# SiLU gate with loads and stores on one DMA ring instead of two

## The chip, the cores and the metric

The kernel runs on one core of a Trainium2 chip. A core has compute engines that work at the same time and wait for one another through semaphores; this kernel uses two of them, ScalarE (ACT in the profile) and VectorE (DVE). SyncE (SP) computes nothing here; it issues transfers. Data moves between the off-chip memory (HBM) and the on-chip memory (SBUF, 128 partitions) by DMA, on 16 DMA engines. A transfer is issued by an instruction of SP or ACT; its packets then stand in a ring that belongs to the issuing engine, and the DMA engines work through the rings. The profile calls the ring of SP q1 and that of ACT q10.

The metric is the time of one execution on the device, in microseconds (us). The kernel before took 471.0 us (median of three runs, 470.98 to 471.02).

## The reference

The input x has the shape 32 x 512 x 2048 in float32. The last axis is cut into two halves of 1024; the output is SiLU of the first half times the second half.

```python
half_dim = x.shape[-1] // 2
x1, x2 = x[..., :half_dim].copy(), x[..., half_dim:].copy()
silu_x1 = x1 * (1 / (1 + np.exp(-x1)))
return (silu_x1 * x2).astype(np.float32)
```

That is 134.2 MB read, 67.1 MB written, one activation and one multiply for each output element.

## The kernel before

The 32 x 512 rows are taken as 16384 rows of 2048 numbers. A tile is 1024 rows: 128 partitions with K = 8 rows each. So there are 16 tiles; a tile's load is 8 MB (64 KB in one piece for each partition) and its store 4 MB (32 KB in one piece for each partition). The helper `view` (lines 42 and 43) picks tile i of a tensor.

In SBUF there are two input buffers, `xts`, and two output buffers, `ots`; tile i uses number i % 2 of each. ACT overwrites the first half of an input row with its SiLU (line 96), and DVE multiplies the two halves into the output buffer (line 102). Both calls are in `compute`. Most tiles are one activation and one multiply of 128 x 8192 elements. Tile 0 is done in four parts of 2 rows a partition (`FIRST`), and tile 15 in parts of 2, 3 and 3 rows (`LAST`).

The order of the work is written out by hand. Every transfer goes through `move` (line 76), which issues it on the queue that it is given and notes it in `sent`. `load(i)` issues on SP and `store(i, ...)` on ACT. The order in the program is load 0, load 1, and then for each tile i: compute tile i, store tile i, load tile i+2. For tiles 4 to 7 and 12 to 15 (`load_first`) the load stands ahead of the store; for those two queues that changes the order in which the transfers take their semaphores, and not what each queue waits for.

Load i+2 writes the input buffer that multiply i reads, so SP waits for that multiply ahead of it. Store i waits on ACT's queue for the same multiply. Multiply i+2 writes the output buffer that store i reads, so it waits for that store to land. ACT's queue is in order too: the activation of tile i+1 stands behind store i.

Tile 0 is stored in three transfers (`OPENING`): every fourth partition from 0, every fourth from 2, and then every odd one. Tile 15 is stored in three transfers that follow `LAST`. All other stores are one transfer over all partitions. Loads are always one transfer.

The helper `implied` tells the framework that a dependency is already covered by another one. `after` fixes an order in the program without a wait. At the end `settle_all_but` makes SP wait for all transfers but the last, and then the program ends when the last has landed.

Of the kernel before, what the change touches and what calls it, by code (L numbers as in the profile page):

```python
# [1 line left out]

# [4 lines left out]


@with_exitstack
def kernel(  # L10
    ctx: ExitStack,
    tc: tile.TileContext,
    x: bass.AP,
    out: bass.AP,
):


    nc = tc.nc
    P = nc.NUM_PARTITIONS

    x_flat = x.flatten_outer_dims()
    out_flat = out.flatten_outer_dims()
    num_rows, in_cols = x_flat.shape
    half = in_cols // 2
    dt = x_flat.dtype

    K = 8
    FIRST = [2] * (K // 2)
    LAST = [2, 3, 3]
    OPENING = [  # L30
        (slice(0, None, 4), slice(None)),
        (slice(2, None, 4), slice(None)),
        (slice(1, None, 2), slice(None)),
    ]
    RUN = 2
    n_tiles = num_rows // (P * K)

    pool = ctx.enter_context(tc.tile_pool(name="pool", bufs=1))
    xts = [pool.tile([P, K, in_cols], dt, name=f"xt{b}") for b in range(2)]
    ots = [pool.tile([P, K, half], dt, name=f"ot{b}") for b in range(2)]  # L40

    def view(flat, i):
        return flat.rearrange("(g p t k) d -> g t p k d", p=P, t=RUN, k=K)[i // RUN, i % RUN]

    ctx.enter_context(tc.manual_schedule(engines={mybir.EngineType.Activation, mybir.EngineType.DVE}))

    sent = []
    loads, stores, silus, muls = {}, {}, {}, {}

    def implied(later, earlier, reason):  # L50
        for x in later:
            for y in earlier:
                tc.declare_no_dep(x, y, reason=reason)

    def earlier(done, i):
        return [ins for j in range(i % 2, i, 2) for ins in done[j]]

    def after(later, first):
        tc.add_manual_dep(
            later,  # L60
            first.name,
            mybir.DependencyInfo(mybir.DependencyClass.NoSync, mybir.DependencyReason.DATA),
            reason="order in which the transfers take their semaphores",
        )

    def settle_all_but(n, others):
        rest = nc.sync.nop(nofuse=True)
        for ins in sent[:-n] + others:
            tc.add_manual_dep(
                rest.ins,  # L70
                ins.name,
                mybir.DependencyInfo(mybir.DependencyClass.Sync, mybir.DependencyReason.DATA),
                reason="sync sees each earlier transfer land before the last ones",
            )

    def move(queue, out, in_):
        ins = queue.dma_start(out=out, in_=in_).ins  # L77
        sent.append(ins)
        return ins

    def load(i):
        loads[i] = [move(nc.sync, xts[i % 2][:], view(x_flat, i))]
        if i >= 2:
            implied(loads[i], earlier(loads, i), "the multiplies that this load awaits came after those loads")
            implied(loads[i], earlier(silus, i), "the multiplies that this load awaits came after those activations")

    def parts(sizes):
        assert sum(sizes) == K
        return [slice(sum(sizes[:n]), sum(sizes[:n + 1])) for n in range(len(sizes))]

    def compute(i, ot, chunks):
        xt = xts[i % 2]
        silus[i], muls[i] = [], []
        for ks in chunks:
            silus[i].append(
                nc.scalar.activation(  # L96
                    out=xt[:, ks, :half],
                    in_=xt[:, ks, :half],
                    func=mybir.ActivationFunctionType.Silu,
                ).ins  # L100
            )
            muls[i].append(nc.vector.tensor_mul(out=ot[:, ks], in0=xt[:, ks, :half], in1=xt[:, ks, half:]).ins)  # L102
        implied(muls[i], loads[i], "each multiply awaits an activation that came after the load")
        if i >= 2:
            implied(silus[i], earlier(silus, i), "the load that this activation awaits came after those activations")
            implied(silus[i], earlier(muls, i), "the load that this activation awaits came after those multiplies")
            implied(muls[i], earlier(muls, i), "the store that this multiply awaits came after those multiplies")

    def store(i, ot, pieces):
        ov = view(out_flat, i)  # L110
        stores[i] = [move(nc.scalar, ov[ps, ks], ot[ps, ks]) for ps, ks in pieces]

    ALL = slice(None)
    load(0)
    load(1)
    for i in range(n_tiles):
        ot = ots[i % 2]
        last = i == n_tiles - 1
        compute(i, ot, parts(FIRST if i == 0 else LAST if last else [K]))
        pieces = [(ALL, ALL)]  # L120
        if i == 0:
            pieces = OPENING
        elif last:
            pieces = [(ALL, ks) for ks in parts(LAST)]
        load_first = i // 4 % 2
        if load_first and i + 2 < n_tiles:
            load(i + 2)
        store(i, ot, pieces)
        if load_first and i + 2 < n_tiles:
            after(stores[i][0], loads[i + 2][0])  # L130
        if not load_first and i + 2 < n_tiles:
            load(i + 2)
            after(loads[i + 2][0], stores[i][-1])
    settle_all_but(1, muls[n_tiles - 1])


# [1 line left out]
_INS = ['x']  # L138
_OUTS = [((32, 512, 1024), 'float32')]


# [23 lines left out]
```

## Time and profile before

| | |
|---|---|
| time, median of three runs | 471.0 us |
| the profiled execution, first to last instruction (span) | 469.2 us |
| median less span | 1.8 us |
| DVE busy | 139.5 us, 21 multiplies |
| ACT busy | 114.2 us, 21 activations and one table load |
| multiply of a whole tile | 8.69 us |
| activation of a whole tile | 7.03 us |
| ring of SP (loads) | 134.22 MB, 66.4% of the span of 16 engines |
| ring of ACT (stores) | 67.11 MB, 33.2% of the span of 16 engines |
| load, from issue to landing (median) | 42.2 us |
| store of a whole tile, from issue to landing (median) | 42.0 us |

The span is one execution taken by the hardware profiler, from its first to its last instruction; that is the only time that the profile gives of that execution. The chain of waits is the chain of work that ended last, followed back from the end: each step names what released it. In a table by stretches, each row is a stretch of the span, with its length, the busy time of each engine, the mean busy share of the 16 DMA engines, and what they moved in GB/s. There, a DMA packet is counted where it starts, with its whole duration and its whole size. So in a short stretch that holds the start of one packet on each of the 16 engines, the share times the length is the mean duration of a packet, and the GB/s times the length is the size of the 16 packets.

### The profile page before, as it was taken

The numbers are of one execution on the slowest core, as the hardware profiler recorded it, in microseconds if no ns is written. First come the engines' busy times: TensorE is split into PE (matmuls) and PEld (weight loads), VectorE is DVE, ScalarE is ACT, GpSimd is POOL, SyncE is SP. The second block draws the span as 40 slices with busy tenths as digits, with TensorE's granted clock in tenths as the row PEclk, the third lists the DMA queues.
The fourth block names the chain that finished last, engine by engine and source line by source line (L and its number), as shares of the span: only waits on it lengthen the run. The fifth ranks groups of instructions, "written<-read, shape, count | busy, mean of one in ns | idle before, by whom it ended". The sixth has DMA issues, their size and how long they took to land.

```text
span 469.2 us, 156 instructions
## 1 busy us (share of the span) xinstructions
DVE 139.5 (30%) x21; ACT 114.2 (24%) x22; POOL 0.2 (0%) x4
## 2 busy tenths in 40 slices
DVE  0070522407034070330704307042070520605152
ACT  1051405032050410504105050050501405014060
POOL 0000000000000000000000000000000000000000
DMA  8999999999999999999999999999999999999998
GB/s 358 447 447 374 475 402 433 416 492 402 411 439 486 408 402 447 475 419 402 444 439 458 402 436 413 492 402 416 433 486 408 402 447 475 419 402 444 450 402 358
DMA packets 4928, 201.33 MB, mean 429 GB/s; under 512 B 576, under 2 KB 576, under 8 KB 576
## 3 DMA queue, kind: packets, MB, share of 16 engines
q1 hardware_dynamic: 2304, 134.22, 66.4%
q10 hardware_dynamic: 2624, 67.11, 33.2%
HBM read 134.22 MB, written 67.11 MB: 429 GB/s over the span
## 4 chain that ended last, share of the span: by engine, by line
DMA 72%; DVE 14%; ACT 11%; DVEq 1%; issue 0%; SPq 0%
DMA xt<-in_x_dram 72%; DVE ot L102 14%; ACT xt L96 11%; DVEq L160 1%; SPq L77 0%
## 5 line engine op out<-in xcount | busy, mean ns | idle before, releaser
L102 DVE TENSOR_TENSOR ot<-xt 128x8192 f32<-128x8192 f32 (+2 forms) x21 | 139.5, 6659 | 320.8 <-ACT xt L96 320.8
L96 ACT ACTIVATE xt<-xt 128x8192 f32<-128x8192 f32 (+2 forms) x21 | 112.9, 5400 | 341.4 <-DMA xt<-in_x_dram 341.4
L96 ACT ACT_TABLE_LOAD x1 | 1.3, 1283 | 0.7 <-PEq L149 0.7
L149 POOL MEMSET const-bfloat16-1.0<- 128x1 bf16 x1 | 0.1, 102 | 0.0
L149 POOL MEMSET const-uint8-127<- 128x1 uint8 x1 | 0.1, 102 | 0.0
L149 POOL MEMSET const-float32-0.0<- 128x1 f32 x1 | 0.1, 99 | 0.2 <-issue 0.2
L149 POOL MEMSET const-float32-1.0<- 128x1 f32 x1 | 0.1, 99 | 0.0
## 6 DMA issues: line engine op xcount, KB each, us to landing
out_dram<-ot ACTq DMA_DIRECT2D x14, 4096.0 KB, 42.0
out_dram<-ot ACTq DMA_DIRECT2D x3, 1024.0 KB, 12.0
out_dram<-ot ACTq DMA_DIRECT2D x2, 1536.0 KB, 7.9
out_dram<-ot ACTq DMA_DIRECT2D x1, 2048.0 KB, 37.2
xt<-in_x_dram SPq DMA_DIRECT2D x16, 42.2
```

The source lines that it names most:

```text
L96: nc.scalar.activation(out=xt[:, ks, :half], in_=xt[:, ks, :half], func=mybir.ActivationFunctionType.Silu,).ins
L102: muls[i].append(nc.vector.tensor_mul(out=ot[:, ks], in0=xt[:, ks, :half], in1=xt[:, ks, half:]).ins)
L149: nc = _bacc.Bacc("TRN2", target_bir_lowering=False, num_devices=1)
L160: with _tile.TileContext(nc) as tc:
```

## The change

All stores are issued by SP, as the loads are. The ring of ACT isn't used any more. For each tile, store i stands ahead of load i+2 on SP's queue, in the program and in the ring; the alternation by `load_first` is gone. The store of tile 0 is one transfer over all partitions. The three stores of tile 15 stay three.

```diff
-    OPENING = [
-        (slice(0, None, 4), slice(None)),
-        (slice(2, None, 4), slice(None)),
-        (slice(1, None, 2), slice(None)),
-    ]
...
     def store(i, ot, pieces):
         ov = view(out_flat, i)
-        stores[i] = [move(nc.scalar, ov[ps, ks], ot[ps, ks]) for ps, ks in pieces]
+        stores[i] = [move(nc.sync, ov[ps, ks], ot[ps, ks]) for ps, ks in pieces]
...
         pieces = [(ALL, ALL)]
-        if i == 0:
-            pieces = OPENING
-        elif last:
+        if last:
             pieces = [(ALL, ks) for ks in parts(LAST)]
-        load_first = i // 4 % 2
-        if load_first and i + 2 < n_tiles:
-            load(i + 2)
         store(i, ot, pieces)
-        if load_first and i + 2 < n_tiles:
-            after(stores[i][0], loads[i + 2][0])
-        if not load_first and i + 2 < n_tiles:
+        if i + 2 < n_tiles:
             load(i + 2)
             after(loads[i + 2][0], stores[i][-1])
```

## The prediction

> **What bounds the kernel now.** I read the page first: the busy shares, the rings, and the DMA issues.
>
> ```profile
> DVE 139.5 (30%) x21; ACT 114.2 (24%) x22; POOL 0.2 (0%) x4
> ...
> q1 hardware_dynamic: 2304, 134.22, 66.4%
> q10 hardware_dynamic: 2624, 67.11, 33.2%
> HBM read 134.22 MB, written 67.11 MB: 429 GB/s over the span
> ...
> out_dram<-ot ACTq DMA_DIRECT2D x14, 4096.0 KB, 42.0
> ...
> xt<-in_x_dram SPq DMA_DIRECT2D x16, 42.2
> ```
>
> Both compute engines idle more than two thirds of the span, and the packets of the two rings together fill 66.4 + 33.2 = 99.6% of what the 16 DMA engines have. So the DMA engines are the bound. The chain of waits seems to say otherwise, since it puts 25% on DVE and ACT; two tiles of it:
>
> ```profile
> 275.07 0.02 issue
> 275.09 7.04 ACT xt L96
> 282.13 0.02 issue
> 282.15 8.70 DVE ot L102
> 290.85 0.02 issue
> 290.87 42.19 DMA xt<-in_x_dram
> 333.06 0.02 issue
> ```
>
> A load takes 42.19 us from issue to landing, but that is mostly queueing. From landing to landing of tiles of one buffer it is 333.06 - 275.07 = 57.99 us, 29.00 a tile. What the engines can do in 29 us is in the table by stretches (length, DVE, ACT, POOL, clock, DMA share, GB/s):
>
> ```profile
> 1.70:2.50 0.80, 0.00 (x0) 0.31 (x1) 0.00 (x0) 1.00 3.98 1311
> 4.70:33.70 29.00, 8.90 (x4) 7.31 (x4) 0.00 (x0) 1.00 1.00 434
> 31.20:32.00 0.80, 0.80 (x2) 0.00 (x0) 0.00 (x0) 1.00 3.02 1311
> 36.10:36.90 0.80, 0.00 (x0) 0.00 (x0) 0.00 (x0) 1.00 4.10 1311
> ...
> 391.20:420.20 29.00, 8.69 (x1) 6.97 (x2) 0.00 (x0) 1.00 1.00 434
> ...
> 449.20:456.46 7.26, 5.08 (x2) 7.09 (x3) 0.00 (x0) 1.00 1.00 433
> 449.20:449.90 0.69, 0.00 (x0) 0.69 (x1) 0.00 (x0) 1.00 1.75 754
> 458.30:460.15 1.85, 1.85 (x1) 0.00 (x0) 0.00 (x0) 1.00 1.03 436
> ```
>
> The fifth row is the steady state: both rings at work, share 1.00, 434 GB/s. The second is the start, loads 0 and 1 alone on SP's ring: the same 434. The sixth is the end, store 14 alone on ACT's ring: 433. So the DMA engines move the same bytes per us whether rings alternate or one ring runs alone, and whether it reads or writes. From the short rows comes a packet: 1311 GB/s x 0.80 us is 1.05 MB, 16 packets of 64 KB. A load packet takes 3.02 x 0.80 = 2.42 us; the very first, in the first row, 3.98 x 0.80 = 3.18; the one that starts at 36.1, 4.10 x 0.80 = 3.28. A store packet takes 1.75 x 0.69 = 1.21 us.
>
> The packet at 36.1 matters. Store 0 is the first use of ACT's ring; its first part is issued at 33.53, and the load packet then under way takes 0.86 us longer than its neighbours. It happens on all 16 engines (the row's mean is over 16 packets) and does not come back: the row of the steady state has two issues in it (at 406.9) and its mean is full. Once, then, 0.86 us of DMA time is lost.
>
> **The change, part by part.**
>
> *The stores move from ACT's queue to SP's.* ACT loses 20 DMA issues, 17 of about 0.36 us and 1.86 us for the three of tile 0. They cost nothing before: ACT idles 341.4 us for loads. SP gains 18 issues of some 0.33 us, and stands idle otherwise. SP's queue now holds store i ahead of load i+2. Store i waits for multiply i, and so does load i+2 (290.87 in the chain), so the load is later by one issue, 0.33 us, which its place in the ring must cover: next point. Nothing else is queued on SP until the final waits; POOL has no transfer. On ACT, the activation of tile i+1 no longer stands behind store i, but it waits for a load that lands 13 us after that anyway.
>
> *The order in the ring.* Let load i land at time 0. Multiply i ends at 0.02 + 7.04 + 0.02 + 8.70 = 15.8, and store i and load i+2 are issued by 16.5. Ahead of them the ring holds store i-1, 8 packets x 1.21 = 9.68, and load i+1, 8 x 2.416 = 19.33 (12 packets take 29.00 in the second row), which were issued a period earlier. That is 29.01 us of work, so the ring has over 12 us left when new work comes. It doesn't run dry. Load i+2 lands at 2 x 29.01 = 58.0, as now; from issue to landing it stays 42.2. Store i lands about 13.2 + 9.7 = 23 us after issue instead of 42.0, so multiply i+2, which needs the output buffer at about 65, is still covered, by 26 us instead of 7. Per tile 29.01 in place of 29.00: over 14 tiles +0.1 us.
>
> *The opening.* Load 1 has no stores beside it and lands at 22.64 + 19.33 = 42.0 instead of 45.36. Store 0 and load 2 are in the ring by 34.2, 8 us before it ends. Store 0 as one transfer carries the same 4 MB; 32 short completion packets fewer are nothing. The 0.86 us goes if it belongs to starting the second ring, which no longer exists; it stays if it belongs to the first write of the program. The bounds are 0 and -0.86. I take -0.86, because the other slow packet, the first of SP's ring, shows a like size (3.18 - 2.42 = 0.76) where a ring starts and nothing is written; and SP's ring never empties.
>
> *The turns in one ring.* This is what the trace doesn't show: a store behind a load in the same ring (15 times) and a load behind a store (14 times). Load behind load is in the second row: it holds the border between loads 0 and 1 and is still full. Store behind store is between the sixth and last rows. Between rings, direction changes at every packet in the fifth row and costs nothing. Lower bound 0 (a full engine can't gain; the fifth row is no slower than the second); upper bound 0.86 each, the only turn in the trace that lost time, 29 x 0.86 = 25 us. I take 0, the value of the three nearest rows.
>
> Here a rule speaks against the change. The Trainium skill, "DMA: Bandwidth & Descriptors", section "Anatomy of one DMA — SWDGE (gpsimd) path", gives every transfer a fixed cost of about 2 us beside its bytes. If one ring paid that at each of 33 borders with nothing else to fill it, 66 us (an estimate from that page) would come on top. The trace contradicts it for load behind load, where the second row has no gap. The same page, section "Queues, rings and completion order", says that data descriptors of a ring carry no barrier, by which the turns are free.
>
> *The end.* After load 15 lands, store 14 (9.68 us) is in the ring; the first part of tile 15 is issued 4.3 us later (449.06 to 453.35 now), the others at 8.0 and 11.3, and the ring needs them at 9.7, 12.1 and 15.8. Nothing changes; SP then waits for all, as now.
>
> **Sum**, against the profiled execution: 469.2 - 0.86 + 0.1 = 468.4 us of span. The median lies 1.8 us above that span, and I keep that: 470.2 us, -0.16%.
>
> **Rivals.**
>
> *The loss stays (471.1 us).* It came with the first write and not with the second ring: 471.0 + 0.1. For it: a load packet was hit just when the first store came. Against: the like loss where a ring starts.
>
> *Turns cost (slower).* Each of the 29 turns inside the ring leaves the engines idle for c, because what comes next isn't prepared while the last packet of the other direction drains; two rings hid it. The time is 470.2 + 29c. It is 0.2% slower from c = (471.94 - 470.2)/29 = 0.06 us; c = 0.1 gives 473.1 and c = 0.86 gives 495.1. For it: 0.86 was lost at the first turn. Against: direction changes are free at every packet of the fifth row, and borders are free in one direction.
>
> *More than the sum (469.6 us).* Without ACT's ring something outside the span goes too. There are 1.8 us there, unseen by the profile; a third of it gives 470.2 - 0.6. Nothing in the profile speaks for it; its bounds are 468.4 and 470.2.
>
> **How the numbers follow.** The forecast gets 0.52, the loss that stays 0.15, turns 0.22, the gain outside 0.11. 0.2%, 0.94 us, is about what a measurement of this kernel can tell from no change; faster is then below 470.06 and slower above 471.94. The forecast lies 0.14 from the first: of its 0.52 I give 0.10 to faster. Of the turns' 0.22, 0.03 is c below 0.06. So faster 0.10 + 0.11 = 0.21, slower 0.19, same 0.60. The range from 469.3 to 472.6 takes in forecast, staying loss and most of the gain outside, and turns up to c = 0.08; it leaves out dearer turns (0.16) and a larger gain (0.03). The likeliest case's own range is 469.8 to 470.6.
>
> **What would show it.** Right: one ring with 201.33 MB and a share over 99%; landings of loads at 42.0, 71.0, 100.0 and 448.1 us; stores landing about 23 us after issue; per tile 29.0; the packets at 36 us at 2.42; span 468.4. The staying loss would be one load or store packet near 42 us that is 0.8 longer. Turns would show as periods of 29.0 + 2c and as shares below 1.00 in stretches around a border. The prediction is wrong if the ring runs dry after a multiply (SP's store waiting for anything but that multiply), or if the packets themselves take other than 2.42 and 1.21 us once reads and writes come in long runs.

## The result

The changed kernel takes 476.15 us (median of four runs, 476.10 to 476.83) against 471.01 us for the kernel before: the ratio is 1.0114, with a 95% interval of 1.0101 to 1.0126. The forecast was 470.2 with a range to 472.6, so it is 5.1 us slower where 0.8 us of gain was forecast. The profiled execution took 476.83 us with a span of 475.1; the other three have spans of 474.3 to 474.4.

### The profile page after: what moved, and what is told of

Read it like the earlier page. It is cut to its first block, busy times and chain, and to the rows that moved or that the text cites. A ratio compares the mean times of both kernels' runs of the same rounds, so it can differ in the third digit from the quotient of the medians.

```text
span 475.1 us, 153 instructions
## 1 busy us (share of the span) xinstructions
DVE 139.5 (29%) x21; ACT 114.2 (24%) x22; POOL 0.2 (0%) x4
## 3 DMA queue, kind: packets, MB, share of 16 engines
q1 hardware_dynamic: 4896, 201.33, 98.7%
## 4 chain that ended last, share of the span: by engine, by line
DMA 72%; DVE 14%; ACT 11%; DVEq 1%; SPq 1%; ACTq 1%; issue 0%
DMA xt<-in_x_dram 72%; DVE ot L97 14%; ACT xt L91 11%; DVEq L148 1%; SPq L72 1%; ACTq L148 1%
## 6 DMA issues: line engine op xcount, KB each, us to landing
out_dram<-ot SPq DMA_DIRECT2D x15, 4096.0 KB, 23.2
xt<-in_x_dram SPq DMA_DIRECT2D x16, 42.3
```

## The profile after

From the page of the changed kernel, in the order of the lines shown of before:

```profile
DVE 139.5 (29%) x21; ACT 114.2 (24%) x22; POOL 0.2 (0%) x4
...
GB/s 353 441 441 395 466 378 439 441 422 455 406 472 419 406 466 395 439 441 422 450 419 447 436 425 452 395 461 400 428 447 425 447 433 436 439 397 469 414 352 282
...
q1 hardware_dynamic: 4896, 201.33, 98.7%
HBM read 134.22 MB, written 67.11 MB: 424 GB/s over the span
...
out_dram<-ot SPq DMA_DIRECT2D x15, 4096.0 KB, 23.2
...
xt<-in_x_dram SPq DMA_DIRECT2D x16, 42.3
```

The plan of the change came out: one ring, the same bytes, compute untouched, whole stores landing after 23.2 us (forecast: about 23), loads after 42.3. The ring doesn't run dry in the body. Yet the rate is 424 GB/s instead of 429, and the last two slices, 352 and 282, are low. Where the time went is in the chain of waits, in the activations of tiles 1, 3, 5 and so on, each of which starts when its load has landed:

```profile
43.09 7.04 ACT xt L91
...
103.09 7.04 ACT xt L91
...
162.30 7.04 ACT xt L91
...
220.97 7.04 ACT xt L91
...
279.63 7.04 ACT xt L91
...
338.17 7.04 ACT xt L91
...
396.75 7.04 ACT xt L91
...
454.80 1.91 ACT xt L91
```

Two tiles should take 58.0 us. They take 60.00, 59.21, 58.67, 58.66, 58.54, 58.58 and 58.05. Load 1 is already 1.1 us late (42.0 forecast), and load 15 lands at 454.8 instead of the 448.1 forecast: 6.7 us, of which 1.1 come up to load 1 and 5.6 between loads 1 and 15.

The table by stretches shows what is long:

```profile
4.65:33.60 28.95, 8.90 (x4) 7.31 (x4) 0.00 (x0) 1.00 1.00 435
...
38.45:39.30 0.85, 0.00 (x0) 0.00 (x0) 0.00 (x0) 1.00 4.09 1234
43.25:50.50 7.25, 0.35 (x1) 6.87 (x1) 0.00 (x0) 1.00 1.00 434
66.30:66.95 0.65, 0.00 (x0) 0.00 (x0) 0.00 (x0) 1.00 3.49 1512
68.70:69.35 0.65, 0.00 (x0) 0.00 (x0) 0.00 (x0) 1.00 3.75 1512
...
456.00:466.00 10.00, 8.90 (x3) 6.01 (x3) 0.00 (x0) 1.00 0.80 337
471.10:473.60 2.50, 0.00 (x0) 0.00 (x0) 0.00 (x0) 1.00 0.12 49
```

Inside runs of one direction nothing changed: loads alone move 435 GB/s, stores alone 434. The second row holds the 16 last packets of load 1, right ahead of store 0: 4.09 x 0.85 = 3.48 us each, 1.06 longer than 2.42. The fourth and fifth rows hold 15 packets each (1512 GB/s x 0.65 us is 0.98 MB): the last but one and the last packet of load 2. Shares of 3.49 and 3.75 mean 2.42 and 2.60 us: the last load packet ahead of a store is longer, here by 0.18 on average.

The packet records of the whole trace (start, duration and size of each packet) show this at the turns from load to store: 1.06 us on average at the first, 0.07 to 0.20 at the others, and 0.02 at the fifteenth. Elsewhere in the body all but a handful of packets keep 1.21 and 2.42. The long packets are not the same length on all engines: at the second turn they are 0 to 0.5 us over. What decides is the slowest engine, for a tile has landed when all 16 have done their part. By the packets' start times, the first packets of store 0 start within 0.7 us of one another, those of store 13 within 6.0.

The last two rows are the price at the end. After load 15 has landed, the engines that are ahead run dry and wait for tile 15 (share 0.80; before, by the packet records, all engines were busy from there to the last 2 us), and in 2.5 us shortly before the end about two of the 16 still move something. The busy shares say the same: 99.6% of 469.2 us is 467.3 us of packets for each engine before, and 98.7% of 475.1 us is 468.9 after. So of the 5.9 us that the profiled execution is longer, about 2 are longer packets on the average engine and about 4 are engines that stand idle.

## The experiments

Every comparison is with runs of the kernel before on the same chip in the same session (470.86 to 470.99 us).

**Is it the opening?** The store of tile 0 was changed as well as the ring. First the whole store on two rings:

```diff
-            pieces = OPENING
+            pieces = [(ALL, ALL)]
```

> The kernel before with store 0 as one transfer over all partitions, on ACT's ring as before; nothing else. Theory of the turns (a DMA engine loses time each time that a store follows a load in the same ring): this kernel has no such turn before store 14, so 471.0 us, at most 0.5 away. Theory of the opening (the three parts of store 0 kept the 16 engines in step, and the whole store lets them drift apart): about 476, as the changed kernel, with loads' landings later and later.

Measured: 471.02 us, ratio 1.0008 (0.9998 to 1.0017). Then the three parts on one ring:

```diff
-        stores[i] = [move(nc.scalar, ov[ps, ks], ot[ps, ks]) for ps, ks in pieces]
+        stores[i] = [move(nc.sync, ov[ps, ks], ot[ps, ks]) for ps, ks in pieces]
...
-        load_first = i // 4 % 2
+        load_first = False
```

> The changed kernel with store 0 in the three transfers of before, all on SP's ring. Theory of the turns: 15 turns from load to store are still there, 476.1 us, at most 1 away. Theory of the opening: 471.0.

Measured: 475.47 us, ratio 1.0099 (1.0084 to 1.0114). So the opening is cleared: the whole store costs nothing on two rings, and its parts save at most 0.7 us on one.

**Is it writing at all, or many transfers in one ring?**

```diff
+        if i == n_tiles - 1:
+            stores[i] = [move(nc.sync, ov[ps, ks], ot[ps, ks]) for ps, ks in pieces]
+        else:
+            again = x_flat.rearrange("(a p h) d -> a p (h d)", p=P, h=K // 2)
+            stores[i] = [move(nc.sync, ot[:].rearrange("p k d -> p (k d)"), again[i])]
```

> The changed kernel with stores 0 to 14 replaced by reads: in their place in the ring stands a transfer of the same 4 MB in packets of the same size from x into the output buffer, so 15 of the 16 tiles of the output are not written. One ring, as many transfers, no turn to a store before the very end. Theory that the loss is at turns from load to store: 29.0 us a tile and no long packet after the first, so a span of 468.4 and 469.7 to 470.7 us. Rival, that many transfers in one ring cost, whatever their direction: 475 to 476.

Measured: 470.87 us, ratio 1.0000 (0.9991 to 1.0010), span 469.0. The time is 0.2 above the expected upper end, as every packet is a few ns longer. But at the place of the first turn there is nothing; the row answers to 38.45:39.30 above, 2.85 x 0.85 = 2.42 us:

```profile
38.45:39.30 0.85, 0.00 (x0) 0.00 (x0) 0.00 (x0) 1.00 2.85 1234
```

So 34 transfers in one ring cost nothing when all but the last three read. The loss needs stores among the loads.

**Is it a price for each turn?** Loads and stores were cut by partitions and issued in turn, so that there are more turns with shorter runs:

```diff
+    WAYS = [slice(j, None, 4) for j in range(4)]
...
+            for ps in WAYS:
+                stores[i].append(move(nc.sync, ov[ps], ot[ps]))
...
+                loads[i + 2].append(move(nc.sync, xts[i % 2][ps], xin[ps]))
```

> The changed kernel, but stores 0 to 13 and the loads behind them are each cut into four transfers of every fourth partition, issued in turn on SP's ring: a quarter store, a quarter load, and so on. The packets are the same; each DMA engine now goes from load to store 4 times a tile, 57 times instead of 15. Theory of the turns, at a price for each: the changed kernel lost 5.1 us over 15 turns, 0.34 each, so 57 give 476.1 + 42 x 0.34 = 490 us. Rival, long runs (the loss comes from 8 packets of one direction in a row, which let the engines drift apart, and not from the turns): with runs of 2 packets it falls, 471 to 473, with about 1 us for 84 more transfers (at some 0.012 us for a transfer's completion).

Measured: 473.95 us, ratio 1.0065 (1.0050 to 1.0080). With nearly four times the turns the loss is smaller, so a fixed price for a turn is out; the long-run rival came nearer, 1 us below what was measured. The chain of waits shows more than the time does:

```profile
1.17 41.74 DMA xt<-in_x_dram
42.91 0.02 issue
42.92 29.48 DMA xt<-in_x_dram
72.41 0.02 issue
72.42 29.89 DMA xt<-in_x_dram
102.31 0.02 issue
102.33 29.52 DMA xt<-in_x_dram
131.84 0.02 issue
131.86 29.02 DMA xt<-in_x_dram
160.88 0.02 issue
160.90 29.02 DMA xt<-in_x_dram
```

Three tiles lose 0.5, 0.9 and 0.5 us; from then on every tile takes 29.04, to the end. By the packets' start times the engines are then, after 11 turns, 2.0 us apart, and stay so. The same transfers with the stores on ACT's ring are the comparison:

```diff
-                stores[i].append(move(nc.sync, ov[ps], ot[ps]))
+                stores[i].append(move(nc.scalar, ov[ps], ot[ps]))
```

> The quarters of the run with four transfers each, but with the stores on ACT's ring: as many transfers, and each DMA engine alternates one load packet and one store packet. Theory of the run: no loss at the turns, 471.0 plus the completions of 84 more transfers, 0.5 to 1 us, so 471.3 to 472.2; what the one-ring kernel took above this is its loss at turns. Rival, that most of the 3 us of the one-ring kernel with quarters was the price of the extra transfers: 473.5 to 474.5.

Measured: 471.92 us, ratio 1.0022 (1.0012 to 1.0031). The extra transfers cost 0.9 us; the rest of the 3.1, about 2.0 us, is the loss on one ring.

In the kernel before, where nearly every load packet after the start stands alone between two stores, the 16 engines stay 0.6 us apart from the first turn to the end, and no later load packet is longer: turns that all engines make at nearly the same time cost nothing there.

Halves instead of quarters (`slice(j, None, 2)`):

> The changed kernel with stores 0 to 13 and the loads behind them cut into two transfers each (every second partition), issued in turn on SP's ring: runs of 4 packets of one direction, 29 turns from load to store. Theory of the run (a turn from load to store costs more the longer the run of load packets before it): between the 474.0 us measured with runs of 2 and the 476.1 us with runs of 8, so 474.4 to 475.8. Rival, a fixed price for a turn: 476.1 + 14 x 0.34 = 481 us.

Measured: 476.00 us, ratio 1.0109 (1.0079 to 1.0139), with executions from 474.4 to 477.4. That is no fixed price either, but it lies 0.2 us above the range expected and is not clearly less than the changed kernel: the loss differs by 3 us from execution to execution, and how the time grows between runs of 4 and of 8 packets can't be read from these. The packet records of the profiled executions give an order: after the first turn, load packets are longer by 0.0 us in all for each engine in the kernel before, 0.6 with quarters on one ring, 1.1 with halves and 1.9 in the changed kernel.

**Is it the ring?** One ring with the order of packets that two rings give, every eighth partition:

> The same with eight transfers each (every eighth partition): on each DMA engine one store packet, one load packet, and so on, in a single ring. That is the order of packets that the two rings of before give. Theory of the run: nothing is lost at the turns, so the time of before plus about 1 us for 196 more transfers (14 tiles x 14, each with a completion packet of 9 ns on each engine, 1.8 us at most): 471.5 to 473. Rival, the ring itself (two rings hide the turn, one doesn't): 475 or more.

Measured: 720 to 734 us, which says nothing on the question, for it made another bottleneck. A stretch of the steady state:

```profile
200.00:229.00 29.00, 2.57 (x1) 0.00 (x0) 0.00 (x0) 1.00 0.98 262
```

The engines are busy and move 262 GB/s; load packets of 64 KB take 4.47 us (median of the packet records) instead of 2.42. The Trainium skill, "SBUF — State Buffer", section "Door 1: The DMA port swizzle", maps partitions to 16 ports by bits 2 to 4 and 6 of the partition's number. Every eighth partition leaves bit 2 fixed, so by that map eight ports serve 16 engines. The trace agrees with a load packet 1.85 times as long (4.47 against 2.42 us); other causes were not tried.

So the runs were shortened by rows instead, all partitions in every transfer:

```diff
+    WAYS = [slice(j * K // 8, (j + 1) * K // 8) for j in range(8)]
...
+                stores[i].append(move(nc.sync, ov[:, ks], ot[:, ks]))
...
+                loads[i + 2].append(move(nc.sync, xts[i % 2][:, ks], xin[:, ks]))
```

> The changed kernel with stores 0 to 13 and the loads behind them cut by rows: eight transfers each of one row of every partition, issued in turn on SP's ring. Packets are 8 KB and 4 KB; a run of loads before a store is 8 packets but only about 2.5 us long, as one packet of 64 KB. Small packets cost something of their own (8 KB packets took 0.306 us at the end of the kernel before, 1.3% more than an eighth of a 64 KB packet). Theory that the length of the run in time sets the loss: within 1 us of the same kernel on two rings, which runs beside it. Rival, one ring or the number of packets in the run: 3 us or more above it.

> The same eight transfers of one row, with the stores on ACT's ring: the comparison for the kernel on one ring. Both theories: 1 to 3% above the time before from the small packets, 475 to 485 us.

Measured: 481.56 us on one ring, ratio 1.0225 (1.0210 to 1.0240), and 540.5 on two, ratio 1.1484. The second is no comparison. Its queues stopped one another; the waits of SP:

```profile
SPq L73 <- DMA xt<-in_x_dram: 254.0, 70, 14.1
```

SP waited 254 us, not for a multiply but for earlier loads to land. The kernel's transfers take eight semaphores in turn, and 16 transfers a tile use each of them twice; probably that is why the queues waited for each other, which no run tested. The DMA engines are idle at times (share of busy time 0.7 to 0.8 in 17 of 40 slices). So the expectation on the pair is untested. The kernel on one ring says something by itself. Stretches of two tiles, from the start to the end of its body:

```profile
100.00:158.00 58.00, 17.39 (x2) 14.06 (x2) 0.00 (x0) 1.00 1.01 424
158.00:216.00 58.00, 17.38 (x2) 14.06 (x2) 0.00 (x0) 1.00 1.02 426
216.00:274.00 58.00, 17.39 (x2) 14.06 (x2) 0.00 (x0) 1.00 1.02 425
...
390.00:448.00 58.00, 19.58 (x3) 15.97 (x3) 0.00 (x0) 1.00 1.02 425
```

It is even throughout: 8 KB packets take 0.309 us and 4 KB packets 0.159. The first turn, which still comes after whole loads, costs 1.0 us; after it there are no long packets ahead of stores but for two disturbances of 0.7 and 0.5 us, near 150 and 390. A tile needs 29.6 to 29.7 us because of the small packets; that makes most of the 10.6 us. So one ring with a turn every 2.5 us of loading doesn't lose at the turns after the first. Its packets are smaller as well; a single 64 KB load packet between stores on one ring was not measured at full rate.

And the reverse, long runs with another ring beside them:

```diff
+    def ring(i):
+        return nc.scalar if i % 2 else nc.sync
...
-        loads[i] = [move(nc.sync, xts[i % 2][:], view(x_flat, i))]
+        loads[i] = [move(ring(i), xts[i % 2][:], view(x_flat, i))]
...
-        stores[i] = [move(nc.sync, ov[ps, ks], ot[ps, ks]) for ps, ks in pieces]
+        stores[i] = [move(ring(i), ov[ps, ks], ot[ps, ks]) for ps, ks in pieces]
```

> The changed kernel, but the transfers of even tiles go to SP's ring and those of odd tiles to ACT's, each ring in the order store i, load i+2. Every ring has turns from load to store in it, but mostly another ring has packets beside it, and a DMA engine can go on with those. Theory that the turn costs because nothing else can fill it: 471 to 472 us. Rival, that a turn inside a ring costs the engine in any case: 476 or more.

Measured: 490.0 us, but most of it is an error of the design: loads 0 and 1 shared the engines, both landed at about 41.8 us, and nothing was left to move while tile 0 was computed:

```profile
GB/s 380 465 439 86 300 342 455 444 428 423 433 417 439 449 407 428 428 444 412 428 452 399 433 399 457 401 455 428 391 465 404 447 409 404 471 372 484 391 395 333
```

Mended, with `ring(i) if i >= 2 else nc.sync` for the loads:

> Even tiles on SP's ring, odd tiles on ACT's, as in the run that took 490 us, but loads 0 and 1 both on SP's ring, so that load 0 does not share the engines with load 1 at the start. In the trace of the 490 us run, load packets ahead of a store of the other ring were 0.15 us longer on average, after runs of 5 to 7 loads 0.2 to 0.4. Theory of the run: a tile still takes over 29.2 us and the kernel 474 to 480, as a turn after a long run costs between rings too. Rival, that a ring with packets beside it hides the turn and the start alone cost 19 us: 471 to 472.

Measured: 476.89 us, ratio 1.0134 (1.0105 to 1.0163), within the range of the theory of the run. The activations of odd tiles in its chain of waits:

```profile
43.02 7.04 ACT xt L94
...
105.16 7.04 ACT xt L94
...
165.24 7.04 ACT xt L94
...
223.63 7.04 ACT xt L94
...
456.51 0.03 ACT xt L94
```

Two tiles take 62.1, 60.1 and 58.4, and 58.2 on average after that. Not all of the first two is loss: load 1 has the engines to itself, and later loads share them with stores of the other ring, which by an estimate from packets of 2.42 and 1.21 us makes the first of these 2.4 us longer and the second 1.2, and the end not later.

In this kernel a DMA engine does 5 to 7 load packets in a row before a store of the other ring comes, and those turns lose as well (0.08 to 0.37 us on average, by the packet records). Load packets that stand alone between two stores lose 0.02 on average in the same trace, at most 0.41. Another ring does not hide the turn. One ring with short runs doesn't lose after its first turn, two rings with long runs do: after the first turn, what counts is the run of loads ahead of a store, not the ring.

**Is the first turn special?** Before and after lose about 1 us at their first turn. A small store ahead of everything tests whether that is the first write:

```diff
+    zero = pool.tile([P, 64], dt, name="zero")
+    nc.gpsimd.memset(zero[:], 0.0)
+    early = move(nc.scalar, view(out_flat, n_tiles - 1)[:, 0, :64], zero[:])
     load(0)
```

> The kernel before with one small store ahead of everything, on ACT's ring: 64 numbers of each partition, to a place of the output that the last tile's store overwrites. Theory that the 0.86 us at 36 us belongs to the first write, or to the first use of ACT's ring: the long packets at 36 us go and the time falls to 470.0 to 470.5, if the small store hides in the start. Theory of the run: 14 load packets still stand ahead of the first turn, the packets at 36 us stay 0.8 to 0.9 longer, and the time is 471.0 to 471.4.

Measured: 471.12 us, ratio 1.0007 (0.9997 to 1.0016), and in the table by stretches:

```profile
36.00:36.90 0.90, 0.00 (x0) 0.00 (x0) 0.00 (x0) 1.00 3.48 1092
```

That is 15 packets (1092 x 0.90 = 0.98 MB) of 3.48 x 0.90 x 16/15 = 3.34 us, 0.92 over. The small store's packets of 256 bytes went out between the packets of load 0 and landed 22 us after issue, and the long packets stayed. So the loss belongs neither to the first write nor to the first use of ACT's ring, as far as a 256-byte packet counts as a write.

The run that took 490 us says more, though it was not made for this question. There the engines stood idle until store 0 came, did its eight packets, then two packets of load 2, and then the first packet of store 1:

```profile
62.00:62.35 0.35, 0.35 (x1) 0.00 (x0) 0.00 (x0) 1.00 5.63 1498
...
66.40:66.90 0.50, 0.00 (x0) 0.00 (x0) 0.00 (x0) 1.00 6.86 2097
```

The second row holds the second packet of load 2 on all 16 engines: 6.86 x 0.50 = 3.43 us, 1.01 longer than 2.42, after a run of only two. Whole store packets had been written before it. The first row holds the last packets of store 0, ahead of load 2: 5.63 x 0.35 = 1.97 us, 0.76 longer than 1.21; in the changed kernel's trace no store packet is more than 0.02 longer. So the first turn from load to store loses about 1 us with or without a long run ahead of it, and with or without a full store before it. What sets it apart from later turns stays open.

**Does it end?** In the changed kernel the later tiles lost less. Every tile done twice tells a settling from a lasting price:

```diff
-    n_tiles = num_rows // (P * K)
+    here = num_rows // (P * K)
+    n_tiles = 2 * here
...
     def view(flat, i):
+        i = i % here
```

> The changed kernel with every tile computed twice, one pass after the other: 32 loads and 32 stores, 31 turns. Theory of settling (the engines spread until their turns no longer disturb one another): nearly all of the loss of 5.1 us is made in the first 15 turns, so 5 to 7 us above the two-ring kernel done twice. Rival, a lasting price of a run: as much again, 9 to 11 us above it.

> The kernel before with every tile computed twice: the comparison for the one-ring kernel done twice. 16 more tiles at 29.0 us: 471.0 + 464.0 = 935.0 us, at most 1 away, by either theory.

Measured: 940.37 us (939.1 to 945.5) on one ring and 935.67 (935.6 to 935.8) on two, 4.7 us apart with 31 turns, as against 5.1 with 15. By the median the lasting price is out; one of the four executions on one ring, 945.5 us, lies 9.8 above, and its trace was not kept. From the table by stretches of the one-ring kernel, four tiles each:

```profile
45.00:161.00 116.00, 34.77 (x4) 26.64 (x5) 0.00 (x0) 1.00 1.00 429
161.00:277.00 116.00, 34.77 (x4) 27.72 (x4) 0.00 (x0) 1.00 1.00 432
277.00:393.00 116.00, 34.77 (x4) 28.12 (x4) 0.00 (x0) 1.00 1.00 433
393.00:509.00 116.00, 34.77 (x4) 28.12 (x4) 0.00 (x0) 1.00 1.00 434
509.00:625.00 116.00, 34.77 (x4) 28.12 (x4) 0.00 (x0) 1.00 1.00 434
```

These are of the execution of 939.1 us. The rate climbs from 429 to the 434 of before and stays. By the packets' start times the 16 engines are 0.6 us apart at the first turn and 3.9 us from the 17th on, and no more than that at the 31st.

**Is it the distance in HBM?** `RUN = 1` in place of 2 halves the distance from partition to partition, on one ring and on two:

> The changed kernel with RUN = 1: a partition's 8 rows lie directly behind those of the partition before, so a tile is one piece of HBM; partitions are 64 KB apart in x and 32 KB in the output, half of the distance so far. Packets, transfers and their order are the same. Theory that the engines disturb one another by their addresses in HBM: the loss changes by 2 us or more in either direction. Theory that only the run of one direction matters: 4 to 6 us above the two-ring kernel with RUN = 1.

> The kernel before with RUN = 1, the comparison for the one above. By either theory 470.5 to 471.5 us, unless the distance in HBM matters for single packets too.

Measured: 475.49 us on one ring, ratio 1.0097 (1.0082 to 1.0112), and 471.01 on two, ratio 1.0005 (0.9996 to 1.0014). The loss is 4.5 us, about as large as with the double distance. Halving this distance changes little; other layouts were not tried.

## Why the prediction was wrong

- *The bound, and the ring that doesn't run dry*: right. Whole stores land after 23.2 us; SP's waits are for multiplies; stretches of one direction move 434 to 435 GB/s, as read from the start and the end of the profile before.
- *The opening, -0.86 us*: wrong. The loss stayed, as the first rival had it, and measured 1.06 us on average, at the last packet of load 1. The reason that I gave, a ring being started, is refuted: in the changed kernel only SP's ring exists, and it had long been running. The rival's reason, the first write, doesn't hold either: not for small writes, and in the run of 490 us not for whole store packets.
- *The turns in one ring, 0 each*: wrong, and this step decided. I took the value of the nearest rows, and they were rows of the wrong thing: borders without a change of direction, and changes of direction after a single load packet. A change of direction after eight load packets was in none of them. The only row that had one was the first turn of before, after some 14 load packets, and it had lost 0.86; I had put it down to the start of a ring. It was a warning and not a measure: a first turn costs about 1 us even after two load packets, and the later turns of the trace after cost 0.02 to 0.20 on the average engine. On the slowest engine they add up: the trace after has 5.6 us between loads 1 and 15. With the opening that is the whole error: 468.4 + 1.1 + 5.6 = 475.1 us of span.
- *The rival "turns cost"* had the side and the place right. By its formula 476.15 means c = (476.15 - 470.2)/29 = 0.2 us. Its mechanism needs mending in three points: in the changed kernel only the turns from load to store lose, not the 14 back; a second ring doesn't hide them; and it isn't a price for each turn, since quarters with 57 turns lost less and doubling the turns added nothing to the median.
- *The rule of a fixed cost for each transfer*: the section that the prediction names is on transfers issued by GpSimd, and here SP issues them. 34 transfers in one ring, of which only the last three write, took 470.9 us, so nothing of it is seen at borders of one direction.
- *The end*, costed at no change: nearly so in the profiled execution. From the last load's landing to the end it is 475.1 - 454.8 = 20.3 us against 469.2 - 449.1 = 20.1. But the ring did run dry there on the engines that were ahead; they wait for the tile that the slowest one completes.

So the loss came from where the change put eight store packets behind eight load packets on every engine, in place of one behind one. In the kernel done twice it ends when the engines have spread out, and the time of a kernel is that of its slowest engine, so the spread is lost once. What makes the packet long, what is special in the first turn, and whether the spread is what ends the loss, is not settled: the engines stop at 2.0 us apart in one kernel and at 3.9 in another, and in the changed kernel's own trace they were 3.5 apart at the fourth turn and went on to 6.0. That the order of packets makes the loss after the first turn and that it settles is shown; the mechanism inside the DMA engines or the memory is not.

## What to carry to other kernels

Two issuing queues don't add bandwidth, but they fix the order of packets: with loads on one ring and stores on the other, and both filled, each DMA engine alternated packet by packet here, and no long run of loads came ahead of a store after the start. When a term of a sum is taken from rows of the trace, look for the row with the same neighbours, not only the same operation; one odd packet that has them is a reason to test, though not yet a price. And a loss over 15 repeats need not be a price for each: look whether the periods shrink before multiplying.

## What the runs showed of the hardware

- The first turn from load to store made 64 KB load packets 0.7 to 1.3 us longer on average, on one ring or two, after 15 or 16 load packets and once after two (1.01). At later turns in the changed kernel they were 0 to 1.1 us longer after a run of eight; after a run of one, in the kernel before, they were not longer. A turn from store to load cost nothing in the changed kernel; the first one in the run of 490 us made store packets 0.76 longer.
- With quarters the loss ended after three tiles (11 turns), with the engines 2.0 us apart; with whole tiles done twice after about 17 turns, at 3.9 us.
- The Trainium skill, "DMA: Bandwidth & Descriptors", section "Issuing engines are not separate DMA queues", says that issuing from several engines only saves the issuing time. Here SP's issues had time to spare, and two rings were still 5.1 us (1.1%) faster, through the order of packets; the measurement decides.
- Transfers of every eighth partition moved 262 GB/s instead of 434. Packets of 8 KB and 4 KB gave 425.
